# Four projection blocks done last, their input kept in DRAM, and the feed-forward operands built at other places and partly on GpSimd

## The chip, the core and the metric

The kernel runs on one core of one Trainium2 chip. Its time is device time in microseconds (us), the median of three runs. The engines are TensorE (PE in the profile; PEld is its weight load), VectorE (DVE), ScalarE (ACT), GpSimd (POOL) and SyncE (SP), whose queue issues the DMAs.

## The reference

One layer over 2048 tokens of width 1024, in float32:

```
hn = rms_norm(h);  q, k, v, u = hn @ W_in + b_in      # 512 | 128 | 128 | 512 columns
attn = sliding_window_gqa(rotary(q), rotary(k), v)    # window 128, 8 heads, sinks
y    = gelu(s5_ssm(u));  ssm = y * sigmoid(y @ w_glu + b_glu)
h = h + concat(rms_norm(attn), rms_norm(ssm)) @ W_out
h = h + conv_ffn(rms_norm(h))                         # up 1024 -> 2*2816, conv(3), silu*val, down
out = rms_norm(h)
```

The state-space part scans over time in 32 groups of 16 channels, which the kernel takes two at a time: 16 calls of `ssm`.

## The kernel before

Every float32 factor is kept as a rounded high part and the rest, the low part (`hi`, `lo`), and each product is three matmuls (hi·hi, hi·lo, lo·hi). `split` makes such a pair: a cast on ScalarE (L132) and a subtraction (L115) on VectorE, or on GpSimd where an engine `Q` is given. Tokens go in 16 blocks of 128, or in 8 pairs of blocks.

**Head.** `pass_a(g)` takes one pair: `norm_in` loads, squares, scales and transposes its tokens into `hnT_hi` and `hnT_lo` (L188 to L212, two buffers of each), `proj_u` multiplies them with the u columns of W_in (L213 to L226), and `both_qkv(g-1)` projects the two blocks of the pair before to q, k and v (`proj_qkv`, L230 to L273; matmuls in L239 and L240). For g = 1 to 6 this projects pairs 0 to 5. Among these passes stand the 16 tables and matrices of the state-space part (L511 to L568; matmuls in L546, L552 and L566, the results cast by ScalarE in L567). All results go to DRAM: `us_d`, `qk_d`, `v_d`, and `m_d`, `d_d`, `tb_d` for the matrices.

**Late stage.** After `pass_a(7)` the weights for u are given up and their room taken by the pool `s2` of the state-space part. The loop at L790 projects blocks 12 to 15, with `ssm(0)` after block 12 and `attention(0)` after block 14. Then the q, k, v weights are given up; `ssm(1)` and the load of W_out (`load_wo`) follow, and a loop over the 16 blocks with one attention, at most one more `ssm` each (14 in all, `J0 = 2` are done before it) and one output product (L828). `ssm` loads its matrices and u (L593 to L604), multiplies (L622), scans on VectorE, and multiplies again (L641).

**Feed-forward.** After a stage with gate and output of the state-space part (to some 754 us), all large products use a scheme with 7 products instead of 8 (L1112, 5544 matmuls of 128x512). There are five passes: two token halves of the up product with 11 pairs of steps each, and three groups of the down product with 4 pairs. In each pass 7 *fixed* operands `r0` to `r6` (a hi and a lo tile each, one buffer) stay in SBUF; `fixed` (L1022) builds them one after another from two staging tiles `sg0` and `sg1` of one buffer each: load, differences, `split`. `pair` (L1092) does the 7 products of two steps and, in the last pair of a pass, asks for the next pass's operand n behind product n. The *moving* operands (`sq`, `ath`, `atl`, `xt`, `ln`) are made by casts on ScalarE and subtractions on GpSimd; the results are gathered in `yl` and `sm_`, product 0 by a copy on ScalarE (L1116), the others by additions on VectorE.

A scheduler of the framework orders each engine's instructions, by program order and by when their inputs are ready; each engine then works through its own list in order, and so does SyncE with the DMAs. `tc.issue_after(x)` adds an order behind x.

## Time and profile before

| | |
|---|---|
| median of 3 runs | 2121.41 us (2120.86 to 2127.72) |
| profiled execution, its own time | 2117.64 us |
| its span | 2115.8 us |
| TensorE busy | 1987.8 us, 94% of the span |
| VectorE, GpSimd, ScalarE busy | 1619.4, 1096.4, 1037.7 us |
| DMA | 335.51 MB, mean 159 GB/s |
| mean granted TensorE clock | 0.974 of full speed |

TensorE is busy nearly everywhere, so the time is its work plus what it stands idle, plus what it loses where the granted clock is at its lower level. Busy shares are averages: the stretches in which TensorE stands, and what it then waits for, are read from the views by window, the waits and the timelines. Times in the views count from the start of the span.

### The profile page before, as it was taken

The page shows a single profiled execution, that of the slowest core. Times are in us where ns is not written, and L with a number is a line of the kernel's source. Part 1 is how long each engine was busy: PE and PEld are TensorE (multiplying, and loading weights), DVE is VectorE, ACT ScalarE, POOL GpSimd, SP SyncE. Part 2 cuts the span into 40 slices and gives each one's busy share as a digit, 9 for nine tenths or more (in the row PEclk, how much of TensorE's full clock was granted, in tenths as well). Part 3 has the DMA queues.
Part 4 walks back from the last instruction along what each step waited for, and adds up shares of the span by engine and source line. Part 5 has one row for each costly group of instructions (what it writes and reads, how often), then busy time and mean ns, then how long its engine had stood idle before and what let it go on. Part 6 is the DMA issues. An engine that isn't in the chain of part 4 may idle for free.

```text
span 2115.8 us, 29745 instructions
## 1 busy us (share of the span) xinstructions
PE 1987.8 (94%) x10121; PEld 1682.4 (80%) x10121; DVE 1619.4 (77%) x2544; ACT 1037.7 (49%) x2162; POOL 1096.4 (52%) x1110
## 2 busy tenths in 40 slices
PE   7999987999899989999999989999999798999997
PEld 6888976998888878888888778888887576887775
DVE  5877347887766777777777987777779779859887
ACT  5676337786745554444544554544445323224332
POOL 1657315553522235555555645544545577867773
PEclk9999988999999999999999999999999998999999
DMA  7576478888646863232242432232333656555352
GB/s 213 168 264 243 148 219 268 255 251 240 174 139 200 234 204 100 60 100 80 70 141 69 138 96 85 70 103 68 112 98 111 210 194 221 216 182 199 130 169 100
DMA packets 304622, 335.51 MB, mean 159 GB/s; under 512 B 92070, under 2 KB 237910, under 8 KB 302934
## 3 DMA queue, kind: packets, MB, share of 16 engines
q1 hardware_dynamic: 304470, 333.60, 49.4%
q8 instruction: 81, 1.33, 0.3%
q14 instruction: 71, 0.58, 0.1%
HBM read 214.14 MB, written 119.41 MB: 158 GB/s over the span
## 4 chain that ended last, share of the span: by engine, by line
PE 44%; DVE 12%; issue 4%; DMA 2%; POOL 2%; ACT 1%; DVEq 0%; POOLq 0%; SPq 0%; ACTq 0%
PE ps L1112 16%; PE pz L1112 15%; PE pi L1112 6%; PE po L1112 6%; DVE yl L115 2%; DVE sums L115 2%; DMA sg<-in_w_down_dram 1%; DVE sg L115 1%; DVE r4l L115 1%; DVE r0l L115 1%; DVE pp L118 1%; DVE r3l L115 1%; DVE px L118 0%; DVE r2l L115 0%; DVE r5l L115 0%
## 5 line engine op out<-in xcount | busy, mean ns | idle before, releaser
L115 POOL TENSOR_TENSOR rs<-rs,mhalf 128x1 f32<-128x1 f32 x80 | 50.1, 632 | 218.2 <-DVE rs L112 217.6
L118 DVE SCALAR_TENSOR_TENSOR pp<-yl,cw,pp 128x512 f32<-128x512 f32 x176 | 131.9, 749 | 37.0 <-ACT pp L1204 36.4
L1204 ACT ACTIVATE pp<-yl,cb,cw 128x512 f32<-128x512 f32 x88 | 69.0, 784 | 58.8 <-DVE yl L115 57.7
L1209 ACT ACTIVATE xh<-pp 128x512 f32<-128x512 f32 x88 | 52.6, 597 | 90.5 <-DVE pp L118 89.2
L118 DVE SCALAR_TENSOR_TENSOR rs<-rs 128x1 f32<-128x1 f32 x160 | 62.1, 396 | 23.3 <-POOL rs L115 21.3
L115 POOL TENSOR_TENSOR ln<-sums,ln 128x512 fp32r<-128x512 f32 (+1 forms) x43 | 58.6, 1364 | 37.5 <-ACT ln L132 32.8
L115 POOL TENSOR_TENSOR xt<-sums,xt 128x512 fp32r<-128x512 f32 (+1 forms) x39 | 51.9, 1331 | 49.6 <-ACT xt L132 48.7
L115 POOL TENSOR_TENSOR sq<-sums,sq 128x512 fp32r<-128x512 f32 (+1 forms) x42 | 59.5, 1416 | 33.5 <-ACT sq L132 32.0
L218 PE MATMUL pz<-hnT_lo,wu_h 128*128 128x256 f32 x256 | 73.0, 289 | 3.5 <-DVE hnT_lo L115 3.5
L115 DVE TENSOR_TENSOR yl<-pz,yl 128x512 f32<-128x512 f32 x66 | 45.3, 686 | 39.7 <-PE pz L1112 36.8
L115 POOL TENSOR_TENSOR atl<-sums,atl 128x512 fp32r<-128x512 f32 (+1 forms) x40 | 56.2, 1406 | 33.4 <-ACT atl L132 33.4
L218 PE MATMUL pz<-hnT_hi,wu_h 128*128 128x256 f32 x256 | 71.9, 289 | 1.0 <-ACT hnT_hi L132 1.0
L218 PE MATMUL pz<-hnT_hi,wu_l 128*128 128x256 f32 x256 | 72.4, 286 | 0.0
L115 POOL TENSOR_TENSOR ath<-sums,ath 128x512 fp32r<-128x512 f32 (+1 forms) x40 | 59.7, 1493 | 24.1 <-ACT ath L132 24.0
L115 POOL TENSOR_TENSOR vv<-vv 128x255 f32<-128x255 f32 x32 | 26.4, 824 | 81.3 <-DVE vv L115 69.2
L115 DVE TENSOR_TENSOR xh<-px,xh 128x512 f32<-128x512 f32 x88 | 60.4, 687 | 1.8
L115 DVE TENSOR_TENSOR sums<-yt 128x512 f32<-128x512 f32 (+1 forms) x48 | 51.5, 1074 | 13.3 <-POOL xt L115 4.4
L115 DVE TENSOR_TENSOR sg<-sg,sg 128x2048 f32<-128x2048 f32 (+1 forms) x20 | 50.5, 2523 | 10.2 <-DMA sg<-in_w_down_dram 5.4
L115 POOL TENSOR_TENSOR xt<-yt,xt 128x512 fp32r<-128x512 f32 (+1 forms) x28 | 41.5, 1482 | 31.8 <-ACT xt L132 31.8
L239 PE MATMUL pi<-wq_h,hnT_hi 128*128 128x512 f32 x128 | 52.1, 407 | 3.8 <-DVE qf L118 3.8
L115 POOL TENSOR_TENSOR atl<-yh,atl 128x512 fp32r<-128x512 f32 (+1 forms) x29 | 40.7, 1405 | 27.6 <-ACT atl L132 27.6
L115 POOL TENSOR_TENSOR ath<-yh,ath 128x512 fp32r<-128x512 f32 (+1 forms) x29 | 41.3, 1425 | 26.1 <-ACT ath L132 26.1
(1270 smaller groups left out, 7772.4 us busy)
## 6 DMA issues: line engine op xcount, KB each, us to landing
xh<-h_d SPq DMA_DIRECT2D x48, 512.0 KB, 3.9
yt<-in_w_up_dram SPq DMA_DIRECT2D x44, 512.0 KB, 4.1
yh<-in_w_up_dram SPq DMA_DIRECT2D x44, 512.0 KB, 3.8
act_d<-xh SPq DMA_DIRECT2D x44, 512.0 KB, 3.3
h_d<-yl SPq DMA_DIRECT2D x32, 512.0 KB, 4.1
qk_d<-qx SPq DMA_DIRECT2D x16, 768.0 KB, 3.3
sg<-h_d SPq DMA_DIRECT2D x12, 1024.0 KB, 6.1
sg<-in_w_down_dram SPq DMA_DIRECT2D x12, 1024.0 KB, 5.7
```

The source lines that it names most:

```text
L115: (eng or V).tensor_tensor(out=o, in0=x, in1=y, op=op)
L118: V.scalar_tensor_tensor(out=o, in0=x, scalar=s, in1=y, op0=o0, op1=o1)
L218: E.matmul(out=pu, lhsT=l["u"][:, k, cs], rhs=r[:, k, :], start=n == 0, stop=n == 3 * KT - 1)
L239: E.matmul(out=pq, lhsT=l[:, k, ts], rhs=r["q"][:, k, 0:512], start=st, stop=sp_)
L1112: E.matmul(out=b, lhsT=l[:, k], rhs=r[:, k], start=m == 0, stop=m == 3 * kh - 1)
L1204: S.activation(out=v, in_=u[s_][:, o + 2:o + 2 + HF], func=AF.Identity, scale=w2, bias=cb[:, fc_:fc_ + 1])
L1209: S.activation(out=x, in_=v, func=AF.Silu)
```

## The change

- Pairs 0 to 3 are projected to q, k and v among the passes as before. Pairs 4 and 5 are not: their `hnT` tiles are written to DRAM (`hn_d`, four DMAs of 1 MB) and read back (`hn_back`, four DMAs of 1 MB) into the buffers that pairs 6 and 7 leave. The late loop projects pairs 6, 7, 4, 5, with `ssm(0)` to `ssm(3)` after blocks 13, 14, 15 and 8, and `attention(0)` after block 9. The block loop then has 12 calls of `ssm`, not 14.
- In `proj_qkv` all low parts are made on GpSimd; the differences of v have a DMA of their own (15 more), and the v of blocks 7 and 12 are copied on GpSimd, since their successors come much later or earlier.
- Small tiles (`wshift`, `yshift`) and longer `yl`, `sm_` tiles move the tiles of five pools from byte offset 0 to 32 within 64; the operands `r0` to `r6`, W_out and the moving operands from `oa` stand at 32 already.
- `fixed` makes the low parts of `r1` and `r3` on GpSimd (in all but the first build). In a pass's last pair only operands 0 to 3 of the next are asked for, and operands 4 to 6 behind products 1 to 3 of the next pass's first pair.

```diff
     def proj_qkv(b, hi, lo):
-        en = V if b >= NB - 2 else Q
+        en = Q
...
+    LATE = (4, 5)
+
+    def hn_back(g):
+        hnT[g] = [xa.tile([P, KT, 2 * P], F32R, name="hnT_" + x) for x in ("hi", "lo")]
+        for i, t in enumerate(hnT[g]):
+            Y.dma_start(out=f(t), in_=hn_d[g - LATE[0], i])
+
     def pass_a(g):
 
         hnT[g] = norm_in(g)
-        if 0 < g < NB // 2 - 1:
+        if 0 < g <= LATE[0]:
             both_qkv(g - 1)
         proj_u(g, *hnT[g])
+        if g in LATE:
+            for i, t in enumerate(hnT.pop(g)):
+                Y.dma_start(out=hn_d[g - LATE[0], i], in_=f(t))
...
-    for b in range(NB - 4, NB):
-        proj_qkv(b, *hnT[b // 2])
-        if b == NB - 4:
-            ssm(0)
-            load_ssm(2)
-        elif b == NB - 2:
-            attention_in(0)
-            po0 = attention(0)
+    J0 = 4
+    for i, g in enumerate((6, 7) + LATE):
+        for b in (2 * g, 2 * g + 1):
+            proj_qkv(b, *hnT[g])
+            if b == NB - 1:
+                for c in LATE:
+                    hn_back(c)
+            j = 2 * i + b % 2 - 1
+            if 0 <= j < J0:
+                ssm(j)
+                load_ssm(j + 2)
+            if b == 2 * LATE[0] + 1:
+                attention_in(0)
+                po0 = attention(0)
...
-    ssm(1)
-    load_ssm(3)
     for k in range(4):
         load_wo(k)
-    j = J0 = 2
+    j = J0
...
-    def fixed(load, kh):
+    def fixed(load, kh, les="VQVQVVV"):
...
-                split(hi[:, ks], lo[:, ks], t[:, ks])
+                split(hi[:, ks], lo[:, ks], t[:, ks], {"V": V, "Q": Q}[les[n]])
...
-            if nxt is not None:
+            if nxt is not None and n < 4:
                 nxt.append(next(nxt[0]))
...
-            if late and n < 3:
-                res.append(next(late))
+            if late and 0 < n < 4:
+                with tc.issue_after(mm.ins):
+                    res.append(next(late))
```

**The order on TensorE in the head, around the state-space matrices.** In the kernel before, a pair of matrices (the two L566 rows) stands among projection matmuls (L239):

```order
L239 MATMUL pi<-wq_h,hnT_lo 128x512
L239 MATMUL pi<-wq_h,hnT_hi 128x512
L204 MATMUL pp<-cc,hn 128x128 x4
L239 MATMUL pi<-wq_l,hnT_hi 128x512
L239 MATMUL pi<-wq_h,hnT_lo 128x512
L239 MATMUL pi<-wq_h,hnT_hi 128x512
L566 MATMUL px<-kx,shm 128x128 x4
L566 MATMUL po<-kx,shm 128x128 x4
L239 MATMUL pi<-wq_l,hnT_hi 128x512
L239 MATMUL pi<-wq_h,hnT_lo 128x512
```

After the change, line numbers are 17 higher there (L566 is L583, L204 is L205, L218 is L219, L546 and L552 are L563 and L569). From the last product of pair 3 to the first of pair 6 no projection stands on TensorE; its rows there are u products (192), transposes, and eight of the sixteen tables:

```order
L569 MATMUL po<-cS,w 128x16 x2
L205 MATMUL pp<-cc,hn 128x128 x4
L583 MATMUL px<-kx,shm 128x128 x4
L583 MATMUL po<-kx,shm 128x128 x4
L563 MATMUL px<-cc,w 128x128 x2
L569 MATMUL po<-cS,w 128x16 x2
L205 MATMUL pp<-cc,hn 128x128 x4
L563 MATMUL px<-cc,w 128x128 x2
L569 MATMUL po<-cS,w 128x16 x2
L219 MATMUL pz<-hnT_hi,wu_h 128x256 x2
L205 MATMUL pp<-cc,hn 128x128 x4
```

What moved: 192 matmuls of blocks 8 to 11 (24 of 512 and 24 of 256 columns for each block) left this stretch.

**The order of the DMAs on SyncE at the start of the late stage.** Before, the state-space loads (`ms`, `ct`, `u`) come once u is written:

```order
L261 DMA qk_d<-qx 128x1536
L272 DMA v_d<-vx 128x512
L261 DMA qk_d<-qx 128x1536
L674 DMA x_t<-v_d 128x4x64
L272 DMA v_d<-vx 128x512
L261 DMA qk_d<-qx 128x1536
L272 DMA v_d<-vx 128x512
L261 DMA qk_d<-qx 128x1536
L226 DMA us_d<-u_t 1024x1x64 x3
L593 DMA ms<-m_d 128x1024
L594 DMA ms<-d_d 128x2x256
L226 DMA us_d<-u_t 1024x1x64
```

After, the two reads of pair 4's `hnT` stand ahead of the writes of block 12's and 13's results, of u and of the first state-space loads, and they wait for TensorE's last use of pair 6's tiles:

```order
L262 DMA qk_d<-qx 128x1536
L692 DMA x_t<-v_d 128x4x64
L288 DMA hnT_hi<-hn_d 128x2048
L288 DMA hnT_lo<-hn_d 128x2048
L267 DMA v_d<-vx 128x256
L262 DMA qk_d<-qx 128x1536
L227 DMA us_d<-u_t 1024x1x64 x2
L279 DMA v_d<-dx 128x256
L227 DMA us_d<-u_t 1024x1x64
L267 DMA v_d<-vx 128x256
L610 DMA ms<-m_d 128x1024
L611 DMA ms<-d_d 128x2x256
```

What moved: the writes of pairs 4 and 5's v and q, k left this place, and reads of 1 MB each stand at its head; pair 5's reads stand 30 rows further on, behind block 15.

**The order on ScalarE where the second up half begins.** Before, the cast of `r5` (L132) stands four rows ahead of the copy of a finished product 0 (L1116):

```order
L132 CAST ath<-sums 128x512
L132 CAST atl<-yt 128x512
L132 CAST r5h<-sg_12959 128x1024 x2
L132 CAST xt<-yt 128x512
L1204 ACTIVATE px<-sm__12680,cb,cw 128x512
L1209 ACTIVATE xh<-pp 128x512
L1116 COPY yl<-pz 128x512
```

After, the copy (L1138) stands ahead of that cast (L133):

```order
L1138 COPY yl<-pz 128x512
L133 CAST ln<-sums 128x512
L133 CAST sq<-sums 128x512
L133 CAST ath<-sums 128x512
L133 CAST r5h<-sg_13217 128x1024 x2
L133 CAST atl<-yt 128x512
```

What moved: the copy of product 0's result no longer stands behind the cast of `r5`; at the start of the three down passes it still stands behind the casts of `r4` to `r6` or some of them. The `r1` and `r3` subtractions left VectorE's list for GpSimd's.

## Rows read from the trace of the kernel before

**Rows 1.** The page, part 2: TensorE busy tenths in 40 slices of 52.9 us.

```profile
PE   7999987999899989999999989999999798999997
```

**Rows 2.** Windows of 25 us: engine busy (instructions), clock, DMA share, GB/s.

```profile
200.00:225.00 25.00, 25.00 (x194) 23.95 (x193) 13.25 (x29) 13.42 (x28) 11.60 (x19) 1.00 0.66 222
250.00:275.00 25.00, 25.00 (x171) 23.06 (x170) 7.18 (x13) 7.84 (x18) 9.50 (x21) 1.00 0.24 92
275.00:300.00 25.00, 18.98 (x107) 15.71 (x105) 11.62 (x27) 5.38 (x12) 1.96 (x2) 0.86 0.85 240
300.00:325.00 25.00, 18.86 (x112) 16.46 (x112) 20.56 (x53) 11.05 (x37) 2.69 (x4) 0.84 0.89 283
325.00:350.00 25.00, 17.55 (x107) 15.04 (x108) 18.37 (x29) 18.73 (x46) 15.49 (x18) 0.82 1.01 305
350.00:375.00 25.00, 21.27 (x135) 18.93 (x134) 19.79 (x36) 21.31 (x66) 14.76 (x16) 0.86 0.72 217
```

**Rows 3.** Groups by form on ScalarE, 95 to 283 us: busy us, mean ns.

```profile
L222 ACT ACTIVATE u_t<-pz,b_u 128x256 f32<-128x256 f32 x24 | 17.2, 717 | 27.8 <-PE pz L218 27.8
L132 ACT CAST hnT_hi<-pp 128x512 fp32r<-128x512 f32 x20 | 12.0, 602 | 11.6 <-PE pp L204 11.5
L567 ACT CAST dm<-po 128x512 fp32r<-128x512 f32 x8 | 9.7, 1211 | 0.0
L197 ACT ACTIVATE hn<-x_t 128x1024 f32<-128x1024 f32 x9 | 9.6, 1069 | 0.0
```

**Rows 4.** Waits, all engines, 275 to 375 us: total, times, longest.

```profile
POOL vv L115 <- DVE vv L115: 39.8, 8, 25.7
POOL vv L115 <- DMA ms<-m_d: 12.2, 1, 12.2
...
ACT uh L132 <- DMA u<-us_d: 9.6, 2, 5.7
```

**Rows 5.** Timeline of SyncE's queue, 280 to 347 us: start, duration.

```profile
290.81 0.59 SPq L604 DMA_DIRECT2D u<-us_d  x1
...
319.67 1.02 SPq L853 DMA_DIRECT2D xh<-in_w_out_dram  x2
...
337.04 0.53 SPq L853 DMA_DIRECT2D xh<-in_w_out_dram  x1
```

**Rows 6.** Waits of TensorE, 375 to 600 us.

```profile
PE pz L641 <- ACT zh L132: 4.2, 1, 4.2
```

**Rows 7.** Windows in the feed-forward part, columns as in rows 2.

```profile
1200.00:1225.00 25.00, 17.71 (x73) 14.29 (x72) 25.00 (x28) 14.60 (x21) 18.35 (x13) 0.86 0.31 106
1575.00:1600.00 25.00, 25.00 (x112) 20.71 (x111) 21.09 (x30) 14.41 (x23) 12.27 (x13) 1.00 0.15 43
1750.00:1775.00 25.00, 18.72 (x74) 14.20 (x72) 25.00 (x24) 7.64 (x11) 19.94 (x12) 0.92 0.54 167
1925.00:1950.00 25.00, 21.05 (x78) 16.18 (x77) 24.28 (x22) 10.07 (x15) 17.81 (x10) 0.86 0.72 268
```

**Rows 8.** Waits of TensorE, 1195 to 1240 us.

```profile
PE pz L1112 <- ACT yl L1116: 7.3, 1, 7.3
```

**Rows 9.** Waits of TensorE, 1590 to 1700 us.

```profile
PE pi L1112 <- DVE yl L115: 3.7, 1, 3.7
PE pz L1112 <- ACT yl L1116: 2.9, 1, 2.9
```

**Rows 10.** Timeline of ScalarE, 1197 to 1224 us, waits in brackets.

```profile
1203.32 2.00 ACT L132 CAST r4h<-sg 128x1024 fp32r<-128x1024 f32 x2
...
1217.84 1.99 ACT L132 CAST r5h<-sg 128x1024 fp32r<-128x1024 f32 x2 [6.64 <-DMA sg<-h_d]
...
1221.45 0.57 ACT L1116 COPY yl<-pz 128x512 f32<-128x512 f32 x1
```

**Rows 11.** Groups by form on VectorE, 1180 to 1235 us.

```profile
L115 DVE TENSOR_TENSOR r3l<-sg,r3h 128x1024 fp32r<-128x1024 f32 x2 | 2.4, 1210 | 0.0
```

**Rows 12.** Groups by form on GpSimd, 1180 to 1235 us.

```profile
L115 POOL TENSOR_TENSOR atl<-yh,atl 128x512 fp32r<-128x512 f32 x3 | 4.9, 1617 | 2.7 <-ACT atl L132 2.7
```

More of the change, by code (lines that the diff above doesn't have):

```diff
@@ L104, in trunk @@
     h_d = dr.tile([NB, P, D], F32, name="h_d")
+    hn_d = dr.tile([2, 2, P, KT, 2 * P], F32, name="hn_d")
     h2_d = dr.tile([4, P, KT, HF], F32, name="h2_d")
@@ L159, in trunk @@
     t = xa.tile([P, 24 * DH], F32, name="qx", bufs=1)
-    raws += [t[:, i * SW:(i + 1) * SW] for i in range(3)] + [xa.tile([P, SW], F32, name="vx", bufs=1)]
+    raws += [t[:, i * SW:(i + 1) * SW] for i in range(3)] + []
     def load_w(n, k):
@@ L290, in trunk @@
     snk = wp.tile([P, NH], F32, name="snk")
+    wp.tile([P, 8], F32, name="wshift")
     Y.dma_start(out=snk, in_=bcast(a["sinks"][0], NH))
@@ L649, in trunk @@
     gy = pool(ctx, "gy", 2)
+    gy.tile([P, 8], F32, name="yshift", bufs=1)
     s2 = pool(sst, "s2", 2)
@@ L1111, in pair @@
                     for l, r in ((ah, hi), (ah, lo), (al, hi)):
-                        E.matmul(out=b, lhsT=l[:, k], rhs=r[:, k], start=m == 0, stop=m == 3 * kh - 1)
+                        mm = E.matmul(out=b, lhsT=l[:, k], rhs=r[:, k], start=m == 0, stop=m == 3 * kh - 1)
                         m += 1
@@ L1147, in h2_load @@
         return lambda t, i, j: Y.dma_start(out=t, in_=h2_d[hb * 2 + j, :, i * 4:i * 4 + 4, :])
-    b0 = fixed(h2_load(0), 4)
+    b0 = fixed(h2_load(0), 4, "VVVVVVV")
     res = []
@@ L1178, in trunk @@
     ef = pool(ctx, "ef")
-    ef.tile([P, 8], F32, name="shift", bufs=1)
     carry = cc[:, C_MQ:C_MQ + 4 * NF].rearrange("p (f i t) -> p f i t", i=2, t=2)
     def up_place(hb, fx):
-        u = [gy.tile([P, HT + 2], F32, name=nm) for nm in ("yl", "sm_")]
+        u = [gy.tile([P, HT + 16], F32, name=nm) for nm in ("yl", "sm_")]
         for i in range(2):
@@ L1230, in pass_of @@
             if n == 0 and i == 0:
-                late = iter(b0)
-                pair(early, res, cs[0], None, None, first, late)
-            else:
-                pair(ops, res, cs[0], nxt, *cs[2:])
+                ops, pre = early, first
+            else:
+                pre = None
+            pair(ops, res, cs[0], nxt, *(cs[2:] or [None]), pre, builds[n] if i == 0 else None)
             if i == len(pairs) - 3 and nx:
@@ L1265, in dn_place @@
     def dn_place(q, last):
-        h = [gy.tile([P, HT + 2], F32, name=nm)[:, 0:D] for nm in ("yl", "sm_")]
+        h = [gy.tile([P, HT + 16], F32, name=nm)[:, 0:D] for nm in ("yl", "sm_")]
         c = [h[i][:, j * HF:(j + 1) * HF] for i in range(2) for j in range(2)]
```

21 lines of the change are left out of this document (13 added, 8 removed).

## The prediction

> **What bounds the kernel now.** I read the page's busy tenths first [rows 1]: TensorE is at 9 in most slices, so the time is its work plus its holes, and only changes in or beside the holes count. The windows of 25 us then show where the holes lie [rows 2, 7]. The reader should see three things there. Up to 275 us TensorE is busy 25.00 of 25. From 275 to 375 us it is busy 18.98, 18.86, 17.55 and 21.27, and the granted clock there is 0.86, 0.84, 0.82 and 0.86, a mixture of its two levels (2.4 and 1.2 GHz) that follows these gaps. In the feed-forward part 25.00 busy with 112 matmuls is the full pace, 0.223 us for a matmul of 512 columns, and it falls to 17.71, 18.72 and 21.05 where one pass ends and the next begins. The waits say what ends these holes: in the late stage GpSimd, VectorE and ScalarE steps of the state-space chain and their loads [rows 4], in the feed-forward part the gathering of results and the operands [rows 8, 9].
>
> The late stage's hole costs this much: idle 6.0 + 6.1 + 7.5 + 3.7 = 23.3 us, and the missing 0.14, 0.16, 0.18 and 0.14 of the clock over 25 us each, 15.5 us: 39 us in all. The first w_out load is issued at 319.67 [rows 5], and the last projection ends near there. Up to 315 us the hole costs 6.0 + 0.6 x 6.1 idle and 3.5 + 0.6 x 4.0 of clock, 15.6 us; the other 23 us belong to the start of the block loop, after the last projection.
>
> **Part 1, four projection blocks leave the head.** A block is 24 matmuls of 512 columns and 24 of 256. At 0.223 us, and half of it for 256 columns (my estimate from the same row), that is 8.0 us, 32 us for four. The work is not removed; the question is what TensorE does in the two places. In the order after, the stretch from pair 3's last projection to pair 6's first holds 192 u products and 116 smaller matmuls; at 0.112 us each at most, 34.5 us of TensorE. The same stretch has on ScalarE, counted in the order, 10 casts of dm at 1.18 (mean of two forms, one of them in the rows), 8 u_t at 0.717, 11 casts of hnT_hi at 0.602, 6 squares at 1.07 with a read of 0.20 behind each, and some 34 small instructions of mostly 0.24 to 0.62 us, together 13 us: 11.8 + 5.7 + 6.6 + 7.6 + 13 = 44.7 us [rows 3]. So here ScalarE, not TensorE, sets the pace once the projections are gone: TensorE stands about 10 us that it did not stand before. From below the cost is 0 (the scheduler has these casts ready earlier, and ScalarE is busy only 13.42 and 7.84 of 25 in rows 2); from above 25, if half of TensorE's 34.5 us cannot lie beside ScalarE's 44.7 because a bank must be cleared before it is filled again, which also invites the lower clock. I take +10, nearest to the sum of the rows.
>
> **Part 2, the same blocks cover the late stage.** Now eight blocks, 64 us of TensorE, lie beside four state-space chains, where before four blocks lay beside one. The 15.6 us before the last projection are waits of exactly these chains and their first loads [rows 4]: -16. Bounds: 0 if the loads come later as well; -25 if the covered chains also shorten the start of the loop. The start of the loop itself I leave at 0 (-8 to +8): W_out, the v tiles and their splits still need the room that the q, k, v weights leave, so these loads still go out behind the last projection, as at 319.67 and 337.04 [rows 5]; three more state-space calls are done by then, but they were also what filled TensorE there.
>
> **Part 3, the traffic.** Four writes and four reads of 1 MB are 8 MB more. The writes fall between 150 and 225 us, where the DMA share is 0.66 in a window [rows 2], and nobody waits for them. The reads fall into the late stage, whose share is 0.85 to 1.01 at 283 to 305 GB/s: 4 MB at 300 GB/s is 13 us of all engines, and 4 blocks' q, k, v writes of about 1 MB each move there too. They stand at the head of SyncE's queue and wait for TensorE's last use of pair 6's tiles; behind them stand the writes of blocks 12 and 13, of u, and the first state-space loads, whose chain ends with the u load at 290.81 [rows 5]. Block 14's 8 us of TensorE cover that. I take +2, 0 to +10.
>
> **Part 4, the loop.** With two calls of `ssm` fewer in it, two of 14 chances to wait go; the longest such wait is 4.2 us [rows 6]. I take -2, 0 to -5.
>
> **Part 5, the pass boundaries.** At the first up half's end TensorE waits 7.3 us for ScalarE's copy of product 0 [rows 8]: the cast of r5 waits 6.64 us for its load and starts at 1217.84, and the copy at 1221.45 stands behind it [rows 10]. In the order after, the copy stands ahead of this cast, so the wait goes. Late next is the load of r5 itself, for the staging tile comes free only after r4, and r3's low part, ahead of both, is now made by GpSimd; casts of moving operands still stand behind r5. I leave 2 us for that: -5. With the hole the lower clock goes (0.86 in this window, 3.5 us) [rows 7]: -3. Together -8, bounds -11 and +3. At the second half's end [rows 9] the copy still stands behind the cast of r5: 0, -4 to +4. At the three down passes the copy's place is no better, 0 as well before the next term.
>
> Moving r1's and r3's subtractions takes 4 x 1.21 = 4.8 us off VectorE per boundary [rows 11] and puts 4 instructions of 1024 columns on GpSimd. None of that size is on GpSimd in the trace; twice the 512-column row bounds it by 3.2 us [rows 12], and VectorE's 1.21 from below. GpSimd has the room: 18.35 and 19.94 of 25 in the worst windows [rows 7]. But the chain to r4 and r5 grows by 2 x (3.2 - 1.2) = 4 us. VectorE is full in two of the boundary windows (25.00), so there the relief and the longer chain nearly cancel: +2 over four boundaries, -4 to +10. Two rows of this case bear on the price: 128x512 takes GpSimd 1.617 us in the mean here, and VectorE's 128x1024 only 1.21 [rows 11, 12].
>
> On this the Trainium skill speaks, page "SBUF — State Buffer", section "SBUF: two separate sides": VectorE with two SBUF inputs and GpSimd reading SBUF take the same port pair as an exclusive lock, so one of them stands for the whole of the other's instruction. By that rule the move frees no port time and adds the longer GpSimd time to what VectorE must wait for. It would turn the +2 into up to +10; no row here isolates it.
>
> The first pass's changed place of r4 to r6 and the GpSimd low parts of the last two blocks I cost at nothing (-2 to +2): the first is moved by one product, under TensorE at its full pace, the second replaces VectorE work of the same kind while GpSimd is busy 2.69 of 25 [rows 2].
>
> **Part 6, the offsets.** The trace has no pair of like instructions that differ in offset alone. The 768 u products could change by 2% at most, as the spread of like matmuls there, about 2 us. I take -1, -3 to +1.
>
> **The sum.** +10 - 16 + 0 + 2 - 2 - 8 + 2 - 1 = -13. From the profiled execution's 2117.64 us that is 2104.6. The median of the runs lies 3.8 us above it, so the time to be read is 2108.4, say 2108.
>
> **Rivals.**
> First, the head keeps TensorE's pace and the late stage gains more: ScalarE runs ahead in the passes, the +10 becomes 0, the late stage gains 25. For it: ScalarE's low share before. Against: the count above. Sum -32, time 2089.
> Second, on the other side: the head without projections runs at the chain's pace. Each table needs TensorE's transposes, a cast, VectorE, a matmul and the dm casts in turn, from banks with one buffer, and the gaps bring the lower clock as from 275 us on. For it: 18.98 busy and 0.86 in rows 2, where no long block lay ready. Against: the 16 tables have VectorE, GpSimd and ScalarE work for well under the stretch. Price +32 in place of +10, sum +9, time 2130. It decides from 65 us of stretch (34.5 of TensorE plus 30).
> Third, the feed-forward gains nothing: r5's load or the moving casts behind it hold TensorE as long as the copy did, and the port costs its +8. Sum -13 + 8 = -5, or up to +1, time 2117 to 2122. For it: VectorE full at 25.00 across the first boundary [rows 7].
> Fourth, the change does not do what it says: `issue_after` names a matmul, and orders only TensorE's own list, where `fixed` puts nothing. That is so already in the sum; it has no time of its own.
>
> **How the numbers follow.** Forecast 0.45, with its own range of 2096 to 2118; first rival 0.20; second 0.18; third 0.17. A measurement of this kernel cannot tell 0.3%, 6.4 us, from no change. The forecast falls to 0.38 below 2115 and 0.07 within; the first rival is faster; the second is slower by two thirds and within the bound by one; the third is within for 0.10, faster for 0.03 and slower for 0.04. Faster 0.61, same 0.23, slower 0.16. The range, from the first rival's far side to the second's, is 2080 to 2132.
>
> **What the next profile would show.** Part 1 right: holes of some 10 us on TensorE between 190 and 245 us, released by ScalarE (dm, hnT_hi). Part 2 right: no window before the last projection (near 310 us) below 22 busy. Part 5 right: no wait of TensorE for the copy of product 0 above 2 us at the first up half's end, and GpSimd rows for r1 and r3 of 2.4 to 3.2 us. Wrong if TensorE is at its full pace through the head, if the first state-space matmuls stand more than 8 us for their loads behind the reads of `hn_d`, or if the feed-forward part takes longer than before by more than 5 us.

## The result and the profile after

The changed kernel takes 2142.58 us in the median of 5 runs (2136.62 to 2148.0), the kernel before 2121.41 in 5 (2116.68 to 2127.72): 1.0095 times as long, 95% interval 1.0075 to 1.0114. Forecast was 2108. The profiled execution of after took 2147.91 us by its own time, 30 more than that of before, a run at the long end of the spread.

Of these 30 us, 23.0 are there when the feed-forward part begins (777.4 against 754.4 us), and that part takes 1360.2 us in place of 1352.8 (from the start of its first product to that of its last).

**The head and the late stage.** Two windows of before, ahead of those in [rows 2]:

```profile
150.00:175.00 25.00, 23.98 (x166) 21.73 (x165) 18.86 (x41) 18.90 (x57) 17.48 (x30) 1.00 0.67 247
175.00:200.00 25.00, 24.53 (x173) 22.41 (x172) 17.13 (x35) 14.19 (x30) 16.59 (x25) 1.00 0.69 256
```

Windows of after, which answer to them and to [rows 2]:

```profile
150.00:175.00 25.00, 21.42 (x148) 19.27 (x147) 17.04 (x37) 19.92 (x59) 16.27 (x27) 0.96 0.84 273
175.00:200.00 25.00, 21.96 (x155) 20.97 (x155) 15.02 (x37) 14.97 (x31) 15.05 (x22) 0.84 0.82 316
200.00:225.00 25.00, 23.41 (x167) 22.35 (x167) 12.92 (x30) 11.70 (x23) 9.21 (x13) 0.86 0.89 295
250.00:275.00 25.00, 25.00 (x183) 23.68 (x182) 6.15 (x12) 6.80 (x16) 7.61 (x20) 1.00 0.49 158
275.00:300.00 25.00, 25.00 (x149) 22.07 (x148) 11.80 (x22) 5.60 (x14) 10.38 (x18) 1.00 1.04 341
300.00:325.00 25.00, 23.36 (x157) 21.27 (x156) 17.93 (x39) 10.75 (x37) 10.90 (x22) 1.00 0.84 279
325.00:350.00 25.00, 14.89 (x68) 12.02 (x68) 15.61 (x27) 12.56 (x26) 21.27 (x33) 0.67 0.91 288
350.00:375.00 25.00, 17.25 (x96) 14.09 (x94) 13.00 (x24) 16.61 (x44) 11.03 (x8) 0.79 0.98 280
```

The late stage did what was forecast: 275 to 325 us is nearly full, where before lost 6 us a window and the clock. But from 150 us on, where before was nearly full, TensorE is busy 21.42, 21.96 and 23.41 of 25 at a clock of 0.96, 0.84 and 0.86, and the stretch behind the last projection (which now ends at 327 us, before at 316) is worse, 14.89 and 17.25 busy at 0.67 and 0.79. What ends the waits in the head:

```profile
PE px L583 <- DVE kx L116: 3.1, 2, 2.4
PE px L563 <- ACT dm L584: 1.7, 2, 0.9
PE po L569 <- ACT dm L584: 1.2, 2, 0.8
...
PE pz L219 <- ACT hnT_hi L133: 0.7, 1, 0.7
```

They are the chain of the state-space matrices: casts of dm, and kx and hnT_hi, short waits each, on ScalarE and VectorE. The stretch from pair 3's last projection to pair 6's first, which holds no other projection, lasts 51.6 us (168.7 to 220.2). At 200 to 225 us the gaps are 1.6 us and the clock still costs 3.5.

SyncE's queue behind the last projection, which answers to [rows 5]:

```profile
330.98 0.92 SPq L877 DMA_DIRECT2D xh<-in_w_out_dram  x2
...
338.56 0.33 SPq L279 DMA_DIRECT2D v_d<-dx  x1
...
344.04 0.33 SPq L279 DMA_DIRECT2D v_d<-dx  x1
...
349.33 1.14 SPq L692 DMA_DIRECT2D vpad<-v_d  x2
...
355.55 0.35 SPq L877 DMA_DIRECT2D xh<-in_w_out_dram  x1
```

The same load of the v tiles in the kernel before:

```profile
330.59 1.14 SPq L674 DMA_DIRECT2D vpad<-v_d  x2
```

W_out is first loaded at 330.98 us, 11 us later than before, like the last projection. The v tiles are loaded at 349.33, 19 us later than before, behind the last write of v's differences, and the rest of W_out at 355.55, where before had 337.04.

**The feed-forward part.** ScalarE at the first up half's end, which answers to [rows 10]:

```profile
1232.95 1.98 ACT L133 CAST r4h<-sg 128x1024 fp32r<-128x1024 f32 x2
...
1236.55 1.98 ACT L133 CAST r6h<-sg 128x1024 fp32r<-128x1024 f32 x2
1238.44 0.58 ACT L1138 COPY yl<-pz 128x512 f32<-128x512 f32 x1
```

The copy of product 0 (L1138) now stands ahead of r5's cast, and TensorE's wait for it, 7.3 us in [rows 8], is gone. In its place there is a wait for VectorE:

```profile
PE pz L1134 <- DVE yl L116: 5.8, 1, 5.8
```

The low parts on GpSimd take 2.4 to 2.7 us, inside the bounds of the forecast (1.21 to 3.2):

```profile
L116 POOL TENSOR_TENSOR r1l<-sg,r1h 128x1024 fp32r<-128x1024 f32 x2 | 5.4, 2701 | 0.3 <-ACT r1h L133 0.3
...
L116 POOL TENSOR_TENSOR r3l<-sg,r3h 128x1024 fp32r<-128x1024 f32 x2 | 4.8, 2410 | 0.0
```

What was not expected stands in the steady stretches, where nothing waits. Groups of like matmuls between 900 and 1550 us (count, busy us, mean ns):

```profile
L1134 PE MATMUL ps<-r4h,ln 128*128 128x512 f32 x24 | 8.0, 395 | 0.0
...
L1134 PE MATMUL pi<-r5h,ath 128*128 128x512 f32 x24 | 8.0, 395 | 0.0
...
L1134 PE MATMUL pi<-r1h,ath 128*128 128x512 f32 x24 | 7.9, 389 | 0.0
...
L1134 PE MATMUL ps<-r3h,xt 128*128 128x512 f32 x24 | 7.9, 389 | 0.0
```

Those with r0 to r3 last 389 ns, those with r4 to r6 395. From start to start it is 227 ns against 233 in the mean (229 to 238). A window of 250 us holds 1090 matmuls, against 1105 in the kernel before, at full clock and without a gap:

```profile
900.00:1150.00 250.00, 250.00 (x1090) 204.20 (x1089) 192.24 (x274) 113.68 (x181) 129.82 (x144) 1.00 0.29 89
```

r4 to r6 stood 32 bytes past a multiple of 256 before, and now stand at 160: the longer `yl` and `sm_` tiles and the new `yshift` below them moved them by 160 bytes, and the small tile of 32 bytes that was taken out moved them back by 32.

### The profile page after: what moved, and what is told of

It is laid out like the page before. It is cut to its first block, busy times and chain, and to the rows that moved or that the text cites. A ratio compares the mean times of both kernels' runs of the same rounds, so it can differ in the third digit from the quotient of the medians.

```text
span 2146.1 us, 29827 instructions
## 1 busy us (share of the span) xinstructions
PE 2008.6 (94%) x10121; PEld 1686.7 (79%) x10121; DVE 1607.8 (75%) x2510; ACT 1042.2 (49%) x2164; POOL 1148.2 (53%) x1146
## 4 chain that ended last, share of the span: by engine, by line
PE 44%; DVE 8%; issue 4%; DMA 4%; POOL 3%; ACT 1%; POOLq 0%; DVEq 0%; SPq 0%; ACTq 0%
PE ps L1134 16%; PE pz L1134 15%; PE po L1134 6%; PE pi L1134 6%; DMA sg<-in_w_down_dram 1%; DVE yl L116 1%; DVE sums L116 1%; DMA xh<-h_d 1%; DVE sg L116 1%; DVE yt L116 1%; DMA h_d<-yl 1%; DVE pp L119 0%; POOL atl L116 0%; POOL sq L116 0%; POOL xt L116 0%
## 5 line engine op out<-in xcount | busy, mean ns | idle before, releaser
L219 PE MATMUL pz<-hnT_lo,wu_h 128*128 128x256 f32 x256 | 75.1, 297 | 3.5 <-DVE hnT_lo L116 3.5
L219 PE MATMUL pz<-hnT_hi,wu_h 128*128 128x256 f32 x256 | 74.2, 299 | 4.0 <-ACT hnT_hi L133 4.0
L119 DVE SCALAR_TENSOR_TENSOR rs<-rs 128x1 f32<-128x1 f32 x160 | 60.1, 383 | 22.8 <-POOL rs L116 20.6
L116 POOL TENSOR_TENSOR ln<-sums,ln 128x512 fp32r<-128x512 f32 (+1 forms) x43 | 56.5, 1315 | 36.6 <-ACT ln L133 33.1
L219 PE MATMUL pz<-hnT_hi,wu_l 128*128 128x256 f32 x256 | 74.1, 292 | 0.0
L116 POOL TENSOR_TENSOR atl<-sums,atl 128x512 fp32r<-128x512 f32 (+1 forms) x40 | 56.6, 1416 | 30.5 <-ACT atl L133 27.8
L116 DVE TENSOR_TENSOR sums<-yt 128x512 f32<-128x512 f32 (+1 forms) x48 | 58.7, 1226 | 11.0 <-POOL xt L116 4.4
L116 DVE TENSOR_TENSOR sg<-sg,sg 128x2048 f32<-128x2048 f32 (+1 forms) x20 | 50.7, 2534 | 19.7 <-DMA sg<-h_d 10.2
L240 PE MATMUL pi<-wq_h,hnT_hi 128*128 128x512 f32 x128 | 52.9, 414 | 6.9 <-DVE qf L119 6.3
L116 DVE TENSOR_TENSOR yl<-ps,yl 128x512 f32<-128x512 f32 x70 | 47.9, 684 | 13.3 <-PE ps L1134 10.6
L852 PE MATMUL pi<-w_oh,ath 128*128 128x512 f32 x128 | 53.0, 414 | 4.1 <-ACT w_oh L133 3.2
L116 POOL TENSOR_TENSOR xt<-yh,xt 128x512 fp32r<-128x512 f32 (+1 forms) x28 | 43.3, 1548 | 25.3 <-ACT xt L133 25.1
```

The source lines that it names most:

```text
L116: (eng or V).tensor_tensor(out=o, in0=x, in1=y, op=op)
L119: V.scalar_tensor_tensor(out=o, in0=x, scalar=s, in1=y, op0=o0, op1=o1)
L219: E.matmul(out=pu, lhsT=l["u"][:, k, cs], rhs=r[:, k, :], start=n == 0, stop=n == 3 * KT - 1)
L240: E.matmul(out=pq, lhsT=l[:, k, ts], rhs=r["q"][:, k, 0:512], start=st, stop=sp_)
L852: E.matmul(out=po, lhsT=l[:, k, :], rhs=r[k][:, cs], start=n == 0, stop=n == 11)
```

## The experiments

To compare stretches, the table sums over the 25-us windows of one profiled execution TensorE's idle time and the missing share of the clock times 25 us. Profiled executions of one kernel differ by some us (that of the feed-forward edits alone lies 7 us above the median of its runs, that of all but the late pairs 7.5 us below), so differences below 4 us are not used. The windows stand at fixed times, and where a kernel runs later, the same window holds other work; so where it matters two marks in the work are given as well, the end of the last projection and the start of the first feed-forward product.

| us lost | 50-150 | 150-225 | 225-325 | 325-400 | 400-650 |
|---|---|---|---|---|---|
| before | 9.1 | 1.5 | 19.7 | 19.2 | 22.7 |
| after | 15.7 | 16.7 | 1.6 | 32.7 | 22.0 |
| feed-forward edits alone | 7.8 | 1.5 | 20.1 | 24.3 | 23.0 |
| and the v edits | 12.2 | 3.6 | 13.3 | 27.8 | 19.4 |
| all but the late pairs | 14.0 | 4.0 | 14.0 | 29.8 | 22.8 |
| all, r4 to r6 at 32 | 13.1 | 16.7 | 4.2 | 33.1 | 26.7 |
| the same, two ssm back | 12.1 | 16.8 | 4.6 | 36.8 | 13.0 |
| the same, dm on VectorE | 12.6 | 9.7 | 5.8 | 29.2 | 20.3 |
| one late pair | 13.7 | 4.9 | 17.3 | 22.1 | 6.5 |

### The offset of r4 to r6

The changed kernel with r4 to r6 back at 32:

```diff
     ef = pool(ctx, "ef")
+    ef.tile([P, 32], F32, name="shift", bufs=1)
```

> The changed kernel with 128 more bytes ahead of the fixed operands r4 to r6, so that they start 32 bytes past a multiple of 256 as in the kernel before, not 160. Theory A (the start of r4 to r6 within 256 bytes sets the pace of their 2376 matmuls): these fall from a mean of about 234 ns to 227, and the time by 13 to 17 us, to about 2127. Rival B (the pace is lost to other work on SBUF beside these products, such as r1 and r3 on GpSimd or the longer result tiles): they stay at 229 to 238 ns and the time stays near 2142.

Measured: 2132.59 us, 1.0051 (1.0033 to 1.0069), 10 us less where 13 to 17 were expected; the matmuls of r4 to r6 are at 227 ns, and 250 us hold 1105 again:

```profile
900.00:1150.00 250.00, 250.00 (x1105) 207.08 (x1104) 197.20 (x278) 113.70 (x183) 132.08 (x145) 1.00 0.29 90
```

The kernel before with the offset alone; no engine's order changes:

```diff
-    ef.tile([P, 8], F32, name="shift", bufs=1)
+    ef.tile([P, 40], F32, name="shift", bufs=1)
```

> The kernel before with nothing changed but the small tile ahead of r4: 160 bytes in place of 32, which puts r4 to r6 160 bytes past a multiple of 256. Theory A: their matmuls go from 227 to about 234 ns, and the time rises by 13 to 17 us, to about 2136. Rival B: no change within 3 us.

Measured: 2132.77 us, 1.0045 (1.0024 to 1.0066), r4 to r6 at 233 ns:

```profile
900.00:1150.00 250.00, 250.00 (x1092) 204.50 (x1091) 193.04 (x277) 117.16 (x186) 131.44 (x144) 1.00 0.28 88
```

The two agree: theory A holds, and rival B falls. In the traces it is 2376 x 6.2 ns = 14.7 us; the timed runs give 0.45%, 10 us, with 5 to 14 in the interval. Why they give less is not shown.

Then the kernel before with the feed-forward edits and r4, r5, r6 at other starts, by small tiles between them (the first starts with 0, the second with 128):

```diff
-    ef.tile([P, 8], F32, name="shift", bufs=1)
+    pads = {4: 0, 5: 64, 6: 32}
...
+            if n >= 4 and pads[n]:
+                ef.tile([P, pads[n] // 4], F32, name=f"pad{n}", bufs=1)
+                pads[n] = 0
```

> The kernel with the feed-forward edits, with r4, r5 and r6 starting 0, 64 and 96 bytes past a multiple of 256, the operands beside them (r0 to r3 and the moving ones) at 32 as before. Wanted is the mean of each operand's matmuls. If only 160 is bad they stay at 227 ns; if an operand must stand at 32 bytes like the moving operand, all three rise above 229; if 32 bytes within 64 is the rule, 0 and 64 are slow and 96 is not.

> As before with r4, r5 and r6 at 128, 192 and 224 bytes past a multiple of 256. If the pace follows the distance from the moving operand's 32 bytes within 256, 128 and 192 are as slow as 160 (233 ns) and 224 lies between; if only the middle of the 256 bytes is bad, 128 is slow and 192 and 224 are at 227.

| start past a multiple of 256 | 0 | 32 | 64 | 96 | 128 | 160 | 192 | 224 |
|---|---|---|---|---|---|---|---|---|
| mean ns, start to start | 233.5 | 226.8 | 233.2 | 229.1 | 234.0 | 233.1 | 234.2 | 233.3 |

(2126.15 and 2123.66 us, one run each.) With the moving tiles at 32, only 32 is fast, and 96 stands between. So 32 within 64 is not the rule. Last, the moving tiles `ln` and `xt` at 160 as well, by two small tiles in their pool, and r4 to r6 at 160:

```diff
+        oa.tile([P, 32], F32, name="padA", bufs=1)
...
+    oa.tile([P, 32], F32, name="padB", bufs=1)
     ln2 = oa.tile([P, D], F32, name="ln", bufs=1)
...
-    ef.tile([P, 8], F32, name="shift", bufs=1)
+    ef.tile([P, 40], F32, name="shift", bufs=1)
```

> The kernel before with the feed-forward edits, r4 to r6 at 160 bytes past a multiple of 256 and of the moving tiles ln and xt at 160 as well, the others (ath, atl, sq) and r0 to r3 at 32. Theory P (the two operands of a matmul must start alike within 256): r4 to r6 with ln and xt at 227, with ath, atl, sq at 233; r0 to r3 the other way round. Rival Q (the fixed operand alone must stand at 32): r4 to r6 at 233 with all, r0 to r3 at 227 with all.

```profile
L1114 PE MATMUL po<-r5h,ath 128*128 128x512 f32 x24 | 8.0, 396 | 0.0
...
L1114 PE MATMUL pz<-r3h,ln 128*128 128x512 f32 x24 | 8.0, 395 | 0.0
L1114 PE MATMUL pz<-r4h,ath 128*128 128x512 f32 x24 | 8.0, 395 | 0.0
...
L1114 PE MATMUL po<-r5h,ln 128*128 128x512 f32 x24 | 7.9, 390 | 0.0
...
L1114 PE MATMUL pz<-r4h,xt 128*128 128x512 f32 x24 | 7.9, 390 | 0.0
...
L1114 PE MATMUL pz<-r3h,ath 128*128 128x512 f32 x24 | 7.9, 389 | 0.0
```

One run, 2127.93 us. r3 (at 32) is slow with `ln` (at 160) and fast with `ath` (at 32); r4 and r5 (at 160) are slow with `ath` and fast with `xt` and `ln`. From start to start it is about 228 ns alike and 233 unlike. Theory P holds for the starts tried here: the two operands of such a matmul want the same start within 256 bytes. (In the code of L1112 the fixed operand is `rhs` and the moving one `lhsT`.)

### The feed-forward edits alone

The kernel before with `les="VQVQVVV"` and operands 4 to 6 behind the next pass's first pair:

```diff
-                split(hi[:, ks], lo[:, ks], t[:, ks])
+                split(hi[:, ks], lo[:, ks], t[:, ks], {"V": V, "Q": Q}[les[n]])
...
-            if late and n < 3:
-                res.append(next(late))
+            if late and 0 < n < 4:
+                with tc.issue_after(mm.ins):
+                    res.append(next(late))
```

> The kernel before with only the feed-forward edits of the change: r1 and r3 low parts on GpSimd, operands 4 to 6 behind the first pair's products 1 to 3; head, late stage and all offsets as before. The prediction's part 5 has -6 for this (-8 and +2). From the trace of after, in which the feed-forward part took 1360.2 us with some 15 us lost to the slower r4 to r6, I expect -5 to -10 us, about 2113. Rival: the port and the longer chain eat it, within 3 us of 2121.

Measured: 2115.46 us, 0.9963 (0.9948 to 0.9978), 7.5 us less; as expected. The prediction's part 5 had -6. The profiled execution is the slowest of its ten, 2122.37 us, and its feed-forward part takes 1351.0 us; in the twelve other kernels with these edits and r4 to r6 at 32 it takes 1343 to 1350, against 1352.8 before. The low parts on GpSimd and the later operands were not run apart.

The same with the small tiles and longer result tiles, and r4 to r6 kept at 32:

```diff
+    wp.tile([P, 8], F32, name="wshift")
...
+    gy.tile([P, 8], F32, name="yshift", bufs=1)
...
-    ef.tile([P, 8], F32, name="shift", bufs=1)
+    ef.tile([P, 32], F32, name="shift", bufs=1)
...
-        u = [gy.tile([P, HT + 2], F32, name=nm) for nm in ("yl", "sm_")]
+        u = [gy.tile([P, HT + 16], F32, name=nm) for nm in ("yl", "sm_")]
```

> The kernel before with the feed-forward edits, and with the change's small tiles and longer result tiles alone, r4 to r6 kept 32 bytes past a multiple of 256; every engine's order is that of the kernel with the feed-forward edits. Theory K: 2112 to 2118, as without them; the 512-column projections may fall from 229 to 227 ns. Rival L: 2125 to 2137.

Measured: 2114.87 us, 0.9959 (0.9947 to 0.9971). The other pools' offsets cost nothing; rival L falls.

### The late pairs

The projections of pairs 4 and 5 back among the passes, with the late loop of before; everything else of the change kept but the two copies of v on GpSimd, which are then not needed, r4 to r6 at 32:

```diff
-        if 0 < g <= LATE[0]:
+        if 0 < g < NB // 2 - 1:
             both_qkv(g - 1)
...
-    for i, g in enumerate((6, 7) + LATE):
+    for b in range(NB - 4, NB):
+        proj_qkv(b, *hnT[b // 2])
+        if b == NB - 4:
+            ssm(0)
+            load_ssm(2)
+        elif b == NB - 2:
+            attention_in(0)
+            po0 = attention(0)
```

> The changed kernel with r4 to r6 at their old offset and the projections of pairs 4 and 5 back among the passes, with one state-space call beside the late projections and one before the loop, as before; the other edits of the change stay (low parts on GpSimd, differences of v in their own tile and DMA, offsets of the five pools, feed-forward edits). All theories that put the loss on the moved projections: about 2115, as with the feed-forward edits alone, so the move costs 15 to 19 us. Rival J (the low parts on GpSimd, the 15 more DMAs or the pools' offsets cost it): it stays above 2125.

Measured: 2136.96 us, 1.0054 (1.0035 to 1.0073). The expectation missed by 22 us and rival J holds: moving the projections is not the main part of the loss. With them moved it is 1.0051, the same within the intervals. In the head the move costs about what part 1 said; the two windows without and with it:

```profile
150.00:175.00 25.00, 25.00 (x175) 23.10 (x175) 16.81 (x36) 20.39 (x58) 16.52 (x28) 1.00 0.83 261
175.00:200.00 25.00, 22.72 (x163) 21.55 (x162) 13.50 (x27) 12.95 (x29) 14.30 (x22) 0.93 0.64 235
```

```profile
150.00:175.00 25.00, 20.77 (x138) 18.37 (x137) 17.30 (x40) 19.64 (x58) 16.45 (x28) 0.92 0.84 271
175.00:200.00 25.00, 21.68 (x154) 20.75 (x155) 15.47 (x36) 14.72 (x31) 14.91 (x22) 0.84 0.82 316
```

150 to 225 us loses 4.0 without and 16.7 with it, about half of the difference idle time and half the clock; 225 to 325 us gives back 10 (14.0 to 4.2). Counted to the end of the last projection, which comes at 327.7 us with the move and at 317.5 without, it gives back 6 (10.6 to 4.5), for without the move some of what these windows lose lies behind it already. With the move 35 more small matmuls stand ahead of that end, 4 us at most at half of the 227 ns of 512 columns (an estimate), so some 6 us are lost up to there. From there to the first feed-forward product it is 452.2 us with the move and 454.2 without.

The dm casts on VectorE, with the late pairs:

```diff
-            S.copy(out=dm.rearrange(
+            V.tensor_copy(out=dm.rearrange(
```

> The changed kernel with r4 to r6 at their old offset, and the 16 casts of dm (18.9 us of ScalarE in the head) on VectorE. Theory H (in the head without projections ScalarE sets the pace, the prediction's part 1): the head loses 6 to 12 us less between 150 and 225 us, time 2121 to 2127. Rival I (it is the chain through all engines, each with its waits, and the half clock that follows the gaps): under 4 us less, or none.

Measured: 2124.02 us, 1.0 (0.9984 to 1.0015), 0.5% or some 10 us less; the head loses 9.7 in place of 16.7 between 150 and 225 us:

```profile
150.00:175.00 25.00, 25.00 (x187) 23.72 (x187) 22.14 (x48) 19.26 (x61) 15.75 (x27) 1.00 0.92 308
175.00:200.00 25.00, 20.26 (x143) 19.61 (x142) 19.75 (x42) 10.57 (x23) 15.39 (x22) 0.80 0.91 341
```

150 to 175 us is full, 175 to 200 is not. The stretch from pair 3's last projection to pair 6's first falls from 51.6 to 41.4 us. ScalarE is a good part of the pace there, not all of it; and some 6 us of the gain lie in the loop (20.3 against 26.7), where no dm is cast.

Two state-space calls back into the loop:

```diff
-    J0 = 4
+    J0 = 2
```

> The changed kernel with r4 to r6 at their old offset, and only two state-space calls beside the late projections (after blocks 13 and 14), the other 14 in the block loop. Theory E: the stretch from the last projection to the steady loop gets back the work that filled it: the last projection comes some 6 us earlier, the stretch loses about as much less, 2122 to 2130 in all, or 4 to 8 us less than with four. Rival G (the loop is better off with 12): the same or slower, 2132 to 2140.

Measured: 2123.73 us, 0.9998 (0.9986 to 1.001). The size is as theory E had it, the place is not: the last projection ends at 327 us as before this edit, 325 to 400 us loses as much (36.8 against 33.1), and the gain is in the loop (13.0 against 26.7).

One late pair:

```diff
-    LATE = (4, 5)
+    LATE = (5,)
```

> The changed kernel with r4 to r6 at their old offset, and only pair 5 done last (pairs 6, 7, 5); pair 4 is projected among the passes again. Theory E (the moved blocks are taken out of a head that has no idle TensorE time to fill, and the late stage's start of the block loop is a fixed stretch of some 60 us that needs work to fill it, so the gain before the last projection is paid for twice): half the blocks, about half the loss in the head (10 us in place of 20 up to 225 us) and a late stage between the two; time 2122 to 2129. Rival F (one fixed cost of the detour through DRAM or of SyncE's queue): as with both pairs, 2130 to 2135.

Measured: 2109.41 us, 0.993 (0.9906 to 0.9953): both theories missed by over 12 us, this version beats both kernels. The head loses no more than without a late pair (4.9), and the loop loses 6.5 us where all others lose 13 to 27. Its code is that of the version with two late pairs; the order is not.

### What the v edits cost

The feed-forward edits with the v edits, no projection and no offset moved:

```diff
-        en = V if b >= NB - 2 else Q
+        en = Q
...
+                dx = xa.tile([P, 2, NKV, DH], F32R, name="dx", bufs=1)
+                tt_(dv, vlast[c], vlast[c - 1], ALU.subtract, en)
+                split(dx[:, 0], dx[:, 1], dv, en)
+                Y.dma_start(out=v_d[c, :, 2:4], in_=f(dx))
```

> The kernel before with the feed-forward edits, and with the change's handling of v alone (all low parts on GpSimd, differences of v in a tile and a DMA of their own, 15 more DMAs), no projection moved, no offset moved. With the projections moved back the changed kernel still took 2137 us, 21 us more than the feed-forward edits alone (2115). Theory K (the v edits give the head and the late stage another order, with waits that bring the half clock): 2125 to 2137. Rival L (the pools' offsets do it): 2112 to 2119.

Measured: 2127.9 us, 1.0017 (1.0001 to 1.0032), against 0.9963 without them. And only the first two lines of these:

> The kernel before with the feed-forward edits and of the v edits only the last two blocks' low parts on GpSimd. The v edits together took 11 to 12 us more than the feed-forward edits alone. Theory M (the last blocks' low parts on GpSimd delay the start of the block loop): 2121 to 2127. Rival N (the separate differences of v, with their tile and DMA in all 15 blocks, from 75 us on): 2112 to 2118.

Measured: 2115.75 us, 0.9963 (0.9951 to 0.9976). So the low parts on GpSimd cost nothing, and the separate differences of v cost 0.54%, 11.5 us. (With them goes one of the eight staging tiles of the first weight loads, since `vx` is half as long; the last projection ends as early without it.) The last row of the last projection and the first feed-forward product with them, and without:

```profile
315.58 0.28 PE L240 MATMUL ps<-wq_h,hnT_lo 128*128 128x256 f32 x1
...
769.92 0.47 PE L1113 MATMUL pz<-r0h,sq 128*128 128x512 f32 x1
```

```profile
315.40 0.28 PE L240 MATMUL ps<-wq_h,hnT_lo 128*128 128x256 f32 x1
...
757.63 0.48 PE L1112 MATMUL pz<-r0h,sq 128*128 128x512 f32 x1
```

The 12 us fall behind the last projection, where the edits add no more than the last difference of v: in the head TensorE loses more with them (15.8 us against 10.0 from 50 to 225 us), and has made it up by 316 us. Other kernels say the same. In all ten without late pairs the last projection ends between 315.5 and 318.6 us; from there to the first feed-forward product the eight without the v edits take 439 to 445 us, the two with them 454. What differs behind 316 us is the order: the code of the block loop is the same, but TensorE, VectorE, ScalarE and GpSimd work through it in another order. That the order costs the 12 us fits this, but no run shows it by itself. The kernel with the projections back has on every engine the order of this one; it differs in offsets that cost nothing elsewhere, and still the two were measured at 1.0054 and 1.0017. So the v edits stand between 0.5 and 0.9%, and the late pairs between 0 and 0.3%; more these runs don't give.

The low parts of the last two late blocks on VectorE, r4 to r6 at 160:

```diff
-        en = Q
+        en = V if b // 2 == LATE[-1] else Q
```

> The changed kernel with the low parts of the last two projected blocks (10 and 11) made on VectorE, as the kernel before has it for its last two. Theory C (after the last projection at 326.8 us GpSimd needs until 344 us for the low parts and differences, and the room for the v tiles and W_out comes free that much later): the last write of qk_d and v_d comes 6 to 9 us earlier, the loads of the v tiles at about 341 us in place of 349.3, and the time falls by 5 to 9 us. Rival D (the room waits for the state-space loads on SyncE's queue, not for GpSimd): no change within 3 us.

Measured: 2146.58 us, 1.0111 (1.0094 to 1.0128), no gain: theory C falls, and at its first step, for the last write of v_d comes at 346.81 us and not earlier than the 344.04 of after. The v tiles are loaded at 349.92. The last two differences through two tiles, the order unchanged but for one cast on ScalarE, r4 to r6 at 32:

```diff
-                dx = xa.tile([P, 2, NKV, DH], F32R, name="dx", bufs=1)
+                dx = xa.tile([P, 2, NKV, DH], F32R, name="u_t" if c > b else "dx", bufs=4 if c > b else 1)
```

> The changed kernel with r4 to r6 at their old offset, and the last of the differences of v (block 12's, made when block 11's is) in another tile than the one before it; every engine's order stays. Theory R (the start of the block loop waits for the chain of two differences through one tile): the last write of v_d comes 2 to 5 us earlier, the loads of the v tiles too, and the time falls by 2 to 6 us, to 2127 to 2131. Rival S (these loads wait for the state-space loads ahead of them, or TensorE waits for other things there): no change within 2 us.

Measured: 2135.07 us, 1.0053 (1.0036 to 1.0071). The last write comes at 341.80 in place of 344.55, the v tiles' load at 347.67 in place of 349.84, and nothing is won: theory R falls too. What sets the length of the stretch behind the last projection stays open.

### Building on one late pair

W_out at 32 and the gate stage's operands at 32, by two small tiles, no order changed:

```diff
+    wo.tile([P, 32], F32, name="wopad")
...
+            gw.tile([P, 16], F32, name="gwpad", bufs=1)
```

> The kernel with one late pair (2109 us), every engine's order unchanged, with W_out's operands moved from 160 to 32 bytes past a multiple of 256 and the gate stage's operands from 224 to 32. Theory A extended (a fixed operand of 512 columns is fast where it starts like the stationary tiles, 32 here): the 768 output matmuls fall from 231 to 238 ns to 227, 4 to 5 us, time about 2104. Rival: these matmuls are paced by something else, no change within 2 us.

Measured: 2108.84 us, 0.9944 (0.9927 to 0.9962). The output matmuls fall from 233 to between 228 and 230 ns, 3 us over 768 of them; the time is the same as 0.993 within its interval, so the 4 to 5 us expected can't be told from none.

That with dm on VectorE (the edit above):

> The same, and the 16 casts of dm on VectorE. Theory H (ScalarE sets the pace in the head where the projections are gone): with one pair gone the head has little left to win, 0 to 5 us below the kernel without it. Rival: as with two pairs, 6 to 10 us below.

Measured: 2122.76 us, 0.9999 (0.9987 to 1.0012): 14 us more, where 0 to 5 less was expected. The head is better (0.6 lost between 150 and 225 us), the loop is not. Windows of the loop without and with dm on VectorE:

```profile
425.00:450.00 25.00, 25.00 (x178) 23.24 (x177) 20.90 (x45) 19.56 (x64) 10.54 (x14) 1.00 0.88 264
575.00:600.00 25.00, 23.78 (x164) 21.68 (x163) 19.94 (x35) 20.19 (x49) 7.53 (x10) 1.00 0.62 183
600.00:625.00 25.00, 24.42 (x137) 20.67 (x137) 12.07 (x22) 11.00 (x20) 5.92 (x9) 1.00 0.35 101
```

```profile
425.00:450.00 25.00, 20.80 (x135) 18.38 (x135) 20.11 (x41) 16.38 (x52) 13.32 (x16) 0.97 0.80 253
575.00:600.00 25.00, 20.82 (x140) 19.29 (x141) 19.31 (x34) 22.57 (x59) 7.88 (x8) 0.86 0.69 190
600.00:625.00 25.00, 20.83 (x128) 18.79 (x127) 9.35 (x17) 15.13 (x30) 5.75 (x8) 0.93 0.47 123
```

In the second, TensorE is busy 20.80 of 25 where it was full, and the clock is 0.86 and 0.93 in the two last: the loop's code is the same, only the order of its instructions differs, and it loses 26.1 us against 6.2.

And that with the two tiles for the last differences (the edit above) in place of it:

> The kernel with one late pair and W_out aligned (2109 us), with the same edit. Theory R: 2 to 5 us less, 2104 to 2107. Rival S: 2108 to 2110.

Measured: 2119.73 us, 0.998 (0.9965 to 0.9995), 0.36% or some 8 us more, again lost in the loop (19.5 against 6.2), with another order there.

## Why the prediction was wrong

**Part 6, the offsets: wrong, and the term that is shown best.** The prediction took -1 (-3 to +1), as "the trace has no pair of like instructions that differ in offset alone". It looked at the 768 u products and at the five pools whose offsets the change speaks of, and held r4 to r6 for unchanged because they stand at 32 within 64 as before. They moved by 128 bytes, and that is +10 us (5 to 14). In the trace of before the output matmuls (W_out at 160, moving tile at 32) were already slower, 233 ns in the mean from start to start, than the feed-forward ones at 227; that pair was there and was not read.

**The v edits: not priced.** Of them the prediction priced only "the GpSimd low parts of the last two blocks ... at nothing", which was right (0.9963 with and without). The separate differences of v it listed in the change and left out of the sum, at nothing and without a reason; they cost 11.5 us or more, behind the last projection, where they add next to no work.

**Part 1: right in mechanism, and near in size partly by luck.** +10 was forecast for the head without its projections, +12.7 measured between 150 and 225 us. But the +10 was idle time alone; measured are some 6 of idle time and 7 of the clock, which the part had only in its upper bound. The stretch was forecast at 44.7 us, and at 65 by the second rival; it took 51.6. That ScalarE sets the pace holds for half of it and more: its dm casts taken away, 7 us come back and the stretch falls to 41.4. The longest wait, though, is for VectorE's kx, 2.4 us. (The 0.223 us for 512 columns is a slip of reading, since a window also counts matmuls cut by its edges: from start to start it is 0.227, and no term moves by as much as 1 us.)

**Parts 2 to 4: the hole went, but little of that is the move's gain.** From 225 us to the end of the last projection before lost 16.0 us and after 1.6, as forecast (-16). But the kernel with the projections back loses 10.6 there, for a head that runs later, as with the v edits, shortens that hole too. So the step that failed is to count the whole hole as the gain of the move: it is 6, against 12.7 in the head. Behind the last projection 0 was forecast with bounds of 8; to the first feed-forward product after takes 450.3 us and before 438.9, but the kernels with the v edits and no late pair take 454, so the late pairs are not the cause. The loop, at -2, moved by more than that either way with each new order. Part 3's +2 for the traffic was not run apart; 275 to 300 us is full beside the reads. Over all, the late pairs are between -1 and +7 us by the ratios, not the -6 of parts 1 to 4.

**Part 5: right.** -6 forecast, -7.5 measured. The copy's wait went, but not the whole gap: 5.8 us for VectorE came in its place at that boundary. The third rival, no gain there, falls (its sum of -5 gives 2116 us, not 2117). Of the signs of being wrong one came: the feed-forward part of after took 7.4 us longer than before, by the offset.

On the Trainium skill's rule (page "SBUF — State Buffer", section "SBUF: two separate sides"), the exclusive port pair would have made the GpSimd subtractions cost up to +10; the feed-forward edits with them gained 7.5 us, so it did not decide here; what the subtractions alone cost no run shows.

The measured terms: -7.5 (feed-forward), +10 (offset), +11.5 to 20 (v edits), +7 to -1 (late pairs): 2121.4 + 21.2. The largest of them, the v edits, is therefore known as a range only, and the cause of its cost stays open beyond its place, behind the last projection.

## What to carry to other kernels

Where a change shifts tiles, list the start of every TensorE operand within 256 bytes before and after, not only of those it means to shift, and compare like matmuls from start to start; 6 ns on 2376 of them outweighed all else that was done to the feed-forward part. Price every added instruction of a change, also those that only make another edit possible. And where a scheduler orders a dense loop, an edit outside it can reorder it: here the same loop code, in other orders, lost 6 to 27 us, so each step needs a run of its own and no gain can be added up from others.

## What the runs showed of the hardware

A matmul of 128x512 whose fixed and moving operands start alike within 256 bytes went out every 227 ns (both at 32) or 228 (both at 160), unlike every 229 to 234; the traces give no reason. A subtraction of 128x1024 took GpSimd 2.4 to 2.7 us and VectorE 1.21.

The length of a wait does not say by itself what the clock does next. In after three waits of 0.7 to 0.9 us, 2.4 us of idle time in 5.2 us, were followed by the lower of the clock's two levels (1.2 GHz, 0.50) up to 207 us:

```profile
195.00:200.20 5.20, 2.83 (x22) 2.25 (x22) 4.30 (x13) 4.65 (x10) 2.14 (x3) 1.00 0.26 103
200.40:207.00 6.60, 5.69 (x27) 5.35 (x26) 5.83 (x13) 3.49 (x8) 5.24 (x8) 0.50 1.00 343
```

In the kernel with the feed-forward and the v edits a single wait of 2.9 us was followed by the full clock:

```profile
181.97 0.41 PE L547 MATMUL px<-cc,w 128*128 128x128 f32 x2 [2.86 <-DVE w L115]
```

```profile
182.00:200.00 18.00, 17.29 (x134) 16.55 (x135) 10.24 (x22) 9.59 (x20) 11.23 (x18) 1.00 0.51 183
```
